# Windowed attention on one core: two slots for q and k, three for v and output, and a first q loaded as float32 by SyncE

## The chip, the core and the metric

The kernel runs on one core of a Trainium2 chip. The metric is the device time of one execution in microseconds (us). Executions of one kernel agree within about 0.3%; the change turns out to be of about that size, so the timed comparisons use interleaved rounds with a 95% interval. All timed runs quoted here are in the fast state (the record sets apart a slower state of the chip); the one run of a deliberately wrong kernel is a single one, of unknown state. "The span" is the length of the one execution that the profiler recorded. It is about 1.8 us shorter than the time of that execution (951.8 against 953.58 us for the kernel before).

## The reference, cut to what matters

```python
B, S, D = 4, 4096, 1536          # q, k, v: float32 [B, S, D]
W = 64                           # windows of 64 rows; a row attends to its own window only
logits = einsum('bnwd,bnud->bnwu', q_w, k_w) * D ** -0.5
attn = exp(logits - max); attn = attn / attn.sum(-1)
out = einsum('bnwu,bnud->bnwd', attn, v_w)      # float32 [B, S, D]
```

Three float32 inputs of 100.66 MB each are read once, one output of 100.66 MB is written once: 402.65 MB over HBM, whatever the kernel does.

## The kernel before

The 16384 rows are worked off in 32 units of 512 rows. A unit loads q, k and v (3.15 MB each in HBM) through the queue of POOL (GpSimd), which casts to float16 on the way. PE transposes q and k, multiplies them, ACT takes the exponential, PE multiplies with v, ACT and DVE scale the result into an output tile, and POOL stores that tile (3.15 MB). The last unit is cut into three parts (half, quarter, quarter) to shorten the end, and the three stores of its last part go through SP (SyncE).

```python
AHEAD = 2; SLOTS = 4
units = [Unit(i * UR, [(0, 4, 2)]) for i in range(N - 1)]
units.append(Unit((N - 1) * UR, [(0, 2, 2), (2, 3, 1), (3, 4, 1)]))
inp  = tc.tile_pool(name="inp",  bufs=AHEAD + 1)   # three slots each for q, k, v: 12 KB per partition a slot
outp = tc.tile_pool(name="outp", bufs=2)           # two output slots: 24 KB per partition each
...
load_all(units[0]); ...; load_all(units[1])        # q, k, v of a unit, all through POOL's queue
...
probe = consts.tile([16, 16, 192], FP32)           # 12 KB per partition
for ui, u in enumerate(units):
    if ui + AHEAD < N:
        load_all(units[ui + AHEAD])                # q, k, v of the unit two ahead
    n = ui - 12
    if 1 <= n <= 15 and n != 8:                    # 14 small loads, nothing reads them
        nc.gpsimd.dma_start(out=probe[:n, n, :w], in_=qf[0:n, :w])
    for i in range(len(u.parts)):
        for h, et in scores(u, i):                 # transposes, q k^T, exp
            values(u, i, h, et, last)              # et v, scaled into u.o; last part: stores by nc.sync
        if not last:
            store(u, i)                            # nc.gpsimd.dma_start(out <- u.o)
```

Two facts of the built program matter. POOL's instructions run in order, and the loads and stores on its queue share eight completion semaphores in turn, so the ninth transfer is issued only when the first has landed. And an output tile is written again only after its store has landed.

The softmax here doesn't subtract the row's maximum and nothing guards it: scores larger than these inputs give would overflow.

## Time and profile before

| | before |
|---|---|
| time, median of the first 3 runs | 954.06 us (953.35 to 955.11) |
| span of the profiled run | 951.8 us |
| DMA | 9 tenths or more in 39 of 40 slices |
| PE / DVE / ACT / POOL busy | 70% / 45% / 45% / 10% |
| one unit in the steady part | 29.17 us |

From the page of the kernel before: engine totals, the DMA row of the 40 slices (each digit is a tenth of busy share), two of the DMA queues (packets, MB, share of 16 engines), the HBM account, the shares of the chain of waits, and one line of the list of DMA issues (count, KB each, us to landing):

```profile
span 951.8 us, 12993 instructions
...
PE 668.1 (70%) x5624; PEld 439.5 (46%) x5624; DVE 424.8 (45%) x489; ACT 431.0 (45%) x610; POOL 91.6 (10%) x154
...
DMA  9999999999999999999999999999999999999996
...
q0 software_dynamic: 27824, 250.96, 100.6%
q8 instruction: 44, 0.72, 0.3%
...
HBM read 302.07 MB, written 100.66 MB: 423 GB/s over the span
...
DMA 63%; PE 13%; ACT 7%; another core or an unknown queue 7%; DVE 6%; issue 2%; POOL 1%; ACTq 0%; POOLq 0%; DVEq 0%
...
out_dram<-out_sb POOLq DMA_DIRECT2D x31, 3072.0 KB, 44.0
```

The DMA row says what bounds the kernel. The HBM line gives the work: 402.7 MB. The trace records 16 semaphore updates for each DMA. They are read here as one for each of the 16 DMA engines, as its share lands; the trace doesn't name the engine. The loads of v of units 11, 12 and 13 land at 337.25, 366.42 and 395.58 us, so a unit's 12.58 MB (9.44 read, 3.15 written) take 29.17 us, which is 431 GB/s. At that rate 402.7 MB take 934 us, so at most 18 us of the span are not plain transfer. Note the trap in the chain: 47% of it is waiting for output stores, because that is what the compute engines wait for; but as long as the DMA queue is never empty, such waits cost no time.

The same semaphore updates show a second thing. The 16 engines do not stay together: from the first engine's landing to the last engine's, the very first load takes 1.3 us and the store of unit 30 takes 8.0 us (931.00 to 938.99 us).

The end, from the timeline (start us, duration us, engine, line, operation, out<-in; in brackets the idle time before it and what ended it):

```profile
917.87 1.02 PE L199 MATMUL o<-v,et 128*128 128x512 f16 x4
...
931.79 0.69 ACT L205 ACTIVATE out_sb<-o,rs 128x512 f32<-128x512 f32 x1 [14.09 <-DMA out_dram<-out_sb]
931.81 0.75 DVE L207 TENSOR_SCALAR out_sb<-o,rs 128x512 f32<-128x512 f32 x1 [13.60 <-DMA out_dram<-out_sb]
932.53 3.72 PE L199 MATMUL o<-v,et 128*128 128x512 f16 x8 [13.64 <-ACT out_sb L205]
...
937.60 0.54 POOL L214 DMA_DIRECT2D out_dram<-out_sb  x1 [23.07 <-DVE xq L141]
...
943.17 0.54 POOL L214 DMA_DIRECT2D out_dram<-out_sb  x1 [5.03 <-ACT out_sb L205]
...
947.48 1.49 SPq L210 DMA_DIRECT2D out_dram<-out_sb  x3
...
947.92 0.69 ACT L205 ACTIVATE out_sb<-o,rs 128x512 f32<-128x512 f32 x1 [0.47 <-PE o L199]
```

Line 199 is et times v, lines 205 and 207 are the scaling into the output tile, line 214 is a store by POOL and line 210 the last stores by SP. The first values of the last unit are ready at 918.9 us, but ACT and DVE must wait 14 us for an output slot; it comes free when the store of unit 29 lands (931.68 us on the last engine). After that the last unit's stores come as compute delivers them (937.6, 943.2, 947.5 us), and in between the DMA engines have nothing left: the store issued at 937.60 lands on all 16 engines between 942.77 and 942.94 us.

The view of waits gives the total of such waits (us, times, longest):

```profile
DVE out_sb L207 <- DMA out_dram<-out_sb: 48.0, 19, 13.6
...
ACT out_sb L205 <- DMA out_dram<-out_sb: 30.0, 16, 14.1
```

The start, from the timeline:

```profile
1.25 0.68 POOL L79 DMA_DIRECT2D q<-in_q_dram  x1 [0.81 <-POOLq L245]
1.92 0.56 POOL L79 DMA_DIRECT2D k<-in_k_dram  x1
...
12.21 4.37 PE L135 MATMUL tp<-ident,q 128*128 128x128 f16 x40 [12.21 <-DMA q<-in_q_dram]
```

The q load is POOL's first issue; PE starts when q has landed, at 12.2 us; k lands at 19.4 us.

### The profile page before, as it was taken

Reading aid. Unit: us, or ns where it says so; the run is one execution under the profiler, and the core shown is the slowest. Engines: PE = TensorE matmul, PEld = TensorE weight load, DVE = VectorE, ACT = ScalarE, POOL = GpSimd, SP = SyncE. Lnnn points to the kernel's source line nnn. Section 1 sums busy time; section 2 is a strip of 40 time slices with the busy share of each in tenths; the row PEclk is TensorE's granted clock in tenths of the full one; section 3 lists DMA queues with packets and bytes.
Section 4 is the critical chain, followed back from the end, with each engine's and each line's share of the span. In section 5 each row is a group of like instructions: output and inputs, shape, how many; then the busy total and the mean of one; then the engine's idle time right before and its main releaser. Section 6 shows DMA issues by size and latency. Waiting matters only on the chain.

```text
span 951.8 us, 12993 instructions
## 1 busy us (share of the span) xinstructions
PE 668.1 (70%) x5624; PEld 439.5 (46%) x5624; DVE 424.8 (45%) x489; ACT 431.0 (45%) x610; POOL 91.6 (10%) x154
## 2 busy tenths in 40 slices
PE   3777777768677677776676767767768668677644
PEld 3454445435454354553354544445445445344522
DVE  2554544544345443455434554434454345443422
ACT  2555544354444444444544345544354443454423
POOL 2101001010011000100011001100010101010000
PEclk9999989888799798899988889989798998898987
DMA  9999999999999999999999999999999999999996
GB/s 185 218 223 268 283 280 281 241 254 284 282 281 258 241 280 283 282 270 237 269 283 282 278 243 256 282 282 282 255 250 275 282 281 263 249 268 282 280 284 255
DMA packets 28313, 252.57 MB, mean 265 GB/s; under 512 B 2545, under 2 KB 2656, under 8 KB 12256
## 3 DMA queue, kind: packets, MB, share of 16 engines
q0 software_dynamic: 27824, 250.96, 100.6%
q8 instruction: 44, 0.72, 0.3%
q1 hardware_dynamic: 432, 0.79, 0.2%
q14 instruction: 13, 0.11, 0.0%
HBM read 302.07 MB, written 100.66 MB: 423 GB/s over the span
## 4 chain that ended last, share of the span: by engine, by line
DMA 63%; PE 13%; ACT 7%; another core or an unknown queue 7%; DVE 6%; issue 2%; POOL 1%; ACTq 0%; POOLq 0%; DVEq 0%
DMA out_dram<-out_sb 47%; DMA q<-in_q_dram 9%; PE o L199 8%; DMA k<-in_k_dram 7%; PE lt L148 3%; ACT out_sb L205 3%; DVE out_sb L207 3%; PE tp L135 3%; ACT et L174 2%; ACT xk L141 2%; DVE xk L141 2%; DVE xq L141 1%; ACT xq L141 0%; POOL out_dram L214 0%
## 5 line engine op out<-in xcount | busy, mean ns | idle before, releaser
L199 PE MATMUL o<-v,et 128*128 128x512 f16 x762 | 237.6, 420 | 91.2 <-ACT out_sb L205 86.8
L148 PE MATMUL lt<-xq,xk 128*128 128x256 f16 (+1 forms) x1536 | 232.6, 302 | 43.2 <-DVE xk L141 27.9
L207 DVE TENSOR_SCALAR out_sb<-o,rs 128x512 f32<-128x512 f32 x191 | 143.4, 751 | 197.7 <-PE o L199 149.7
L141 ACT COPY xk<-tp 128x1024 f16<-128x1024 f16 (+1 forms) x96 | 123.5, 1287 | 233.8 <-PE tp L135 233.8
L205 ACT ACTIVATE out_sb<-o,rs 128x512 f32<-128x512 f32 x193 | 132.6, 687 | 158.7 <-PE o L199 118.0
L141 DVE COPY xk<-tp 128x1024 f16<-128x1024 f16 (+1 forms) x97 | 123.3, 1271 | 178.6 <-PE tp L135 178.6
L148 PEld LDWEIGHTS <-xk 128*128 128x128 f16 x1536 | 151.9, 108 | 92.3 <-DVE xk L141 41.7
L135 PE MATMUL tp<-ident,k 128*128 128x128 f16 x1536 | 130.8, 239 | 66.4 <-DMA k<-in_k_dram 60.1
L199 PEld LDWEIGHTS <-et 128*128 128x128 f16 x762 | 74.0, 101 | 220.3 <-issue 183.3
L141 DVE COPY xq<-tp 128x1024 f16<-128x1024 f16 (+1 forms) x129 | 152.2, 1255 | 12.6 <-PE tp L135 12.5
L135 PEld LDWEIGHTS <-k 128*128 128x128 f16 x1536 | 113.3, 109 | 78.4 <-DMA k<-in_k_dram 68.3
L135 PE MATMUL tp<-ident,q 128*128 128x128 f16 x1536 | 103.7, 221 | 37.9 <-DVE xq L141 21.8
L141 ACT COPY xq<-tp 128x1024 f16<-128x1024 f16 x64 | 82.1, 1283 | 91.4 <-PE tp L135 91.4
L135 PEld LDWEIGHTS <-q 128*128 128x128 f16 x1536 | 93.2, 99 | 54.4 <-issue 34.6
L174 ACT ACTIVATE et<-lt,zeros 32x128 f16<-32x128 f32 (+1 forms) x256 | 91.6, 358 | 33.0 <-PE lt L148 27.4
L192 DVE RECIPROCAL rs<-sp 128x2 f32<-128x2 f32 (+1 forms) x65 | 10.7, 165 | 133.1 <-PE sp L187 133.1
L214 POOL DMA_DIRECT2D out_dram<-out_sb x33 | 23.8, 720 | 391.2 <-DVE out_sb L207 269.9
L187 PE MATMUL sp<-ones,et 128*128 128x1 f16 x254 | 16.4, 167 | 41.1 <-ACT et L174 41.1
L187 PEld LDWEIGHTS <-et 128*128 128x128 f16 x254 | 14.3, 102 | 61.8 <-ACT et L174 50.3
L79 POOL DMA_DIRECT2D v<-in_v_dram x34 | 23.6, 694 | 180.8 <-DMA out_dram<-out_sb 51.1
L79 POOL DMA_DIRECT2D q<-in_q_dram x34 | 18.6, 546 | 114.1 <-DMA probe<-in_q_dram 53.1
L79 POOL DMA_DIRECT2D k<-in_k_dram x34 | 18.6, 547 | 78.2 <-DMA k<-in_k_dram 37.2
(11 smaller groups left out, 10.1 us busy)
## 6 DMA issues: line engine op xcount, KB each, us to landing
out_dram<-out_sb POOLq DMA_DIRECT2D x31, 3072.0 KB, 44.0
q<-in_q_dram POOLq DMA_DIRECT2D x31, 1536.0 KB, 47.7
k<-in_k_dram POOLq DMA_DIRECT2D x31, 1536.0 KB, 50.8
v<-in_v_dram POOLq DMA_DIRECT2D x31, 1536.0 KB, 51.3
out_dram<-out_sb POOLq DMA_DIRECT2D x1, 1536.0 KB, 5.3
q<-in_q_dram POOLq DMA_DIRECT2D x1, 768.0 KB, 46.9
k<-in_k_dram POOLq DMA_DIRECT2D x1, 768.0 KB, 43.2
v<-in_v_dram POOLq DMA_DIRECT2D x1, 768.0 KB, 46.4
```

What stands on the lines that cost most here:

```text
L79: nc.gpsimd.dma_start(out=dst, in_=rows(src, u.first[i], hi - lo, r))
L135: nc.tensor.transpose(tp[:, (c - c0) * R + r, j, :], src[:, lo + R * j + r, c * P : (c + 1) * P], ident,)
L141: copy(out=dst, in_=tp)
L148: nc.tensor.matmul(lts[h][:, r, :, :], lhsT=kc[:, r, h, :], rhs=qc[:, :, h, :], start=(c == 0 and r == 0), stop=(c == DC - 1), skip_group_ ...
L174: nc.scalar.activation(et[s, :, :, s], lts[h][s, :, :, s], EXP, bias=zeros[s], scale=scale)
L187: nc.tensor.matmul(sp[:, t, 0:1], lhsT=et[:, r, t, :], rhs=ones[:, 0:1], start=(r == 0), stop=(r == R - 1),)
L192: nc.vector.reciprocal(out=rs, in_=sp[:, :, 0])
L199: nc.tensor.matmul(o, lhsT=et[:, r, t, :], rhs=u.v[:, lo + R * h + r, sl], start=(r == 0), stop=(r == R - 1),)
L205: nc.scalar.activation(dst, o, COPY, bias=0.0, scale=rs[:, t : t + 1])
L207: nc.vector.tensor_scalar_mul(dst, o, scalar1=rs[:, t : t + 1])
L214: nc.gpsimd.dma_start(out=rows(of, u.first[i], hi - lo, R), in_=slots(u.o, lo, hi, R))
```

## The change

The intent: input and output slots are redistributed (q and k lose one slot each, output gains one), so that a store that has not landed stops nobody; k and q are reloaded as soon as a unit's scores are done; v is reloaded at the end of a unit for the third unit on, which is the same place in the program's order as before; and the very first load starts earlier, through SP, whose queue the profile lists as hardware_dynamic (POOL's is software_dynamic). This load is written without a cast, so q comes as float32 into an output slot that is still free, and DVE and ACT cast it. The probe loads go.

```diff
-    inp = ctx.enter_context(tc.tile_pool(name="inp", bufs=AHEAD + 1))
+    qkp = ctx.enter_context(tc.tile_pool(name="qkp", bufs=2))
+    vp = ctx.enter_context(tc.tile_pool(name="vp", bufs=3))
-    outp = ctx.enter_context(tc.tile_pool(name="outp", bufs=2))
+    outp = ctx.enter_context(tc.tile_pool(name="outp", bufs=3))
 ...
-    load_all(units[0])
+    raw = outp.tile([P, SLOTS, D], FP32, tag="out_sb", name="raw")
+    nc.sync.dma_start(out=slots(raw, 0, SLOTS, SLOTS), in_=rows(qf, 0, SLOTS, SLOTS))
+    load_all(0, "kv")
 ...
-    for u in units[1:AHEAD]:
-        load_all(u)
+    load_all(1, "qkv")
+    load_all(2, "v")
+    units[0].q = qkp.tile([P, SLOTS, D], FP16, tag="q16", name="q16")
+    for i in range(SLOTS):
+        copy = nc.scalar.copy if i % 2 else nc.vector.tensor_copy
+        copy(out=units[0].q[:, i, :], in_=raw[:, i, :])
 ...
-    probe = consts.tile([16, 16, 192], FP32, name="probe")
-
     for ui, u in enumerate(units):
-        if ui + AHEAD < N:
-            load_all(units[ui + AHEAD])
-        ... the 14 probe loads ...
         for i in range(len(u.parts)):
-            for h, et in scores(u, i):
+            blocks = scores(u, i)
+            if i == 0:
+                load_all(ui + 2, "qk")
+            for h, et in blocks:
                 values(u, i, h, et, last)
             if not last:
                 store(u, i)
+        load_all(ui + 3, "v")
```

More of the change, by code (lines that the diff above doesn't have):

```diff
@@ L26, in __init__ @@
         self.first = [row0 + P * lo for lo, hi, R in parts]
-AHEAD = 2
 SLOTS = 4
@@ L74, in load @@
         if not hasattr(u, name):
-            setattr(u, name, inp.tile([P, SLOTS, D], FP16, tag=name + "16", name=name + "16"))
+            pool = vp if name == "v" else qkp
+            setattr(u, name, pool.tile([P, SLOTS, D], FP16, tag=name + "16", name=name + "16"))
         src = {"q": qf, "k": kf, "v": vf}[name]
@@ L79, in load, with load_all @@
         nc.gpsimd.dma_start(out=dst, in_=rows(src, u.first[i], hi - lo, r))
-    def load_all(u):
-        for i in range(len(u.parts)):
-            for name in "qkv":
-                load(u, i, name)
-    load_all(units[0])
+    def load_all(ui, names):
+        if ui < N:
+            for i in range(len(units[ui].parts)):
+                for name in names:
+                    load(units[ui], i, name)
+    raw = outp.tile([P, SLOTS, D], FP32, tag="out_sb", name="raw")
+    nc.sync.dma_start(out=slots(raw, 0, SLOTS, SLOTS), in_=rows(qf, 0, SLOTS, SLOTS))
+    load_all(0, "kv")
     ident = consts.tile([P, P], FP16, name="ident")
@@ L214, in store @@
         nc.gpsimd.dma_start(out=rows(of, u.first[i], hi - lo, R), in_=slots(u.o, lo, hi, R))
-    probe = consts.tile([16, 16, 192], FP32, name="probe")
     for ui, u in enumerate(units):
-        if ui + AHEAD < N:
-            load_all(units[ui + AHEAD])
-        n = ui - 12
-        if 1 <= n <= 15 and n != 8:
-            w = 128 + 4 * n
-            nc.gpsimd.dma_start(out=probe[:n, n, :w], in_=qf[0:n, :w])
         for i in range(len(u.parts)):
             last = ui == N - 1 and i == len(u.parts) - 1
-            for h, et in scores(u, i):
+            blocks = scores(u, i)
+            if i == 0:
+                load_all(ui + 2, "qk")
+            for h, et in blocks:
                 values(u, i, h, et, last)
```

## The prediction

> **What bounds the kernel now.** The DMA engines. The page's slices show DMA at 9 tenths in 39 of 40 slices, against PE 70%, DVE and ACT 45% of the span. The page's HBM line gives 302.07 MB read plus 100.66 MB written. In the steady part one unit (9.4 MB read, 3.1 MB written) takes 29.17 us between landings, 431 GB/s (worked out from the trace's landing times). The Trainium skill ("DMA: Bandwidth & Descriptors", section "Where 436 GB/s comes from") puts the fabric ceiling at 435 GB/s; this trace agrees to 1%. 402.7 MB at 431 GB/s is 934 us, so at most 18 us of the 951.8 us span can be saved. They lie, by packets and landings: about 3.7 us at the start; the 16 engines drift apart (first to last landing of one DMA grows from 1.3 to 8.0 us), and the last engine decides; after 939 us the queue runs dry twice while the last unit is still being computed.
>
> **That tail is what the change can touch.** The timeline shows unit 31's first value matmuls done at 918.9 us; then ACT waits 14.1 us and DVE 13.6 us for the store of unit 29 to land (931.7 us), because there are only two output slots. PE stands still with them. Stores land 44 us after issue (list of DMA issues), so output slots stall the middle too (chain of waits: 47% on output stores), but there the DMA queue never empties, so that costs nothing.
>
> **What the change does.**
> - Three output slots: unit 31 writes into unit 28's slot, free around 900 us. The 13.6 us stall goes; compute ends about 940-943 us instead of 948.6 us.
> - Two q/k slots, q/k loads issued after a unit's scores: less look-ahead, but about four 3 MB transfers (7.3 us each) stay queued, as a unit computes in 25 us unstalled against 29.2 us of DMA. No steady starvation. The program's order shows that unit 2's q waits for unit 0's transposes only.
> - First q through SyncE as float32: the same 3.1 MB read. It shares the 16 engines with k (same page, "Issuing engines are not separate DMA queues"), so q and k land together at 17-18 us instead of 12.2 and 19.4; then casts of a few us. First transposes about 20-21 us instead of 12.2. Not critical: over 50 us of loads are queued. Data starts about 1 us earlier.
> - The small probe loads (14, under 80 KB) go: about 0.5 us in total.
>
> **Sum.** Slowest DMA engine: 939 us, minus 1 (start), minus 0.5 (probes), plus the last unit's 3.1 MB store 7.3 us, plus about 1 us end = 946 us. Compute: unit 30 ends about 916, the parts of unit 31 take 13, 6 and 6.5 us, last store 2.3 us: about 945. Both meet at a span near 946 us, time about 948 us: 0.6% faster. Range 945 to 951.5 us. Faster by over 2%: 0.02; within 2%: 0.96; slower by over 2%: 0.02.
>
> **What would show it.** Right: no wait of ACT/DVE for output stores near the end, DMA at full share until about 943 us, unit period still 29.2 us, first transposes near 20 us without a hole in the DMA share at 45-60 us.
>
> **What would make it wrong.** A DMA hole after the first loads if unit 0 starts much later; q/k slots released too late, so that PE waits for k and DMA idles; a lower PE clock in the tail; the engines' drift growing beyond 8 us.

## The result, and the profile after

The time is 949.83 us (median of 4 runs, 949.5 to 950.32) against 954.44 us (median of 4): ratio 0.9953, 95% interval 0.9936 to 0.997. Ratios are the mean time of one kernel's fast runs over that of the other's of the same rounds, so not quite the ratio of the medians. The change is 0.5% faster, and clear of noise.

The page after, the lines that answer to those above:

```profile
span 948.6 us, 12985 instructions
...
DMA  9999999999999999999999999999999999999997
...
q0 software_dynamic: 27232, 249.31, 100.2%
q1 hardware_dynamic: 576, 3.93, 1.1%
q8 instruction: 44, 0.72, 0.3%
...
HBM read 301.99 MB, written 100.66 MB: 424 GB/s over the span
...
out_dram<-out_sb POOLq DMA_DIRECT2D x31, 3072.0 KB, 41.9
```

The transfers are the same and the DMA row is as full. The small second queue (q1) now holds the first q (3.15 MB) beside the last stores.

The end of the changed kernel, from the timeline (lines 209, 215, 217 are the former 199, 205, 207; 224 and 220 are the stores):

```profile
927.10 1.02 PE L209 MATMUL o<-v,et 128*128 128x512 f16 x4
...
927.73 0.69 ACT L215 ACTIVATE out_sb<-o,rs 128x512 f32<-128x512 f32 x1 [0.80 <-PE o L209]
928.16 0.75 DVE L217 TENSOR_SCALAR out_sb<-o,rs 128x512 f32<-128x512 f32 x1 [0.72 <-PE o L209]
928.47 3.56 PE L209 MATMUL o<-v,et 128*128 128x512 f16 x8 [0.35 <-ACT out_sb L215]
...
933.39 0.55 POOL L224 DMA_DIRECT2D out_dram<-out_sb  x1 [12.19 <-DVE xq L151]
...
938.62 0.55 POOL L224 DMA_DIRECT2D out_dram<-out_sb  x1 [4.69 <-ACT out_sb L215]
...
942.93 1.49 SPq L220 DMA_DIRECT2D out_dram<-out_sb  x3
...
943.37 0.69 ACT L215 ACTIVATE out_sb<-o,rs 128x512 f32<-128x512 f32 x1 [0.47 <-PE o L209]
```

No wait of 14 us is left: the values of the last unit's first part are scaled as soon as PE delivers them, and the last part's scaling ends at 944.06 us instead of 948.61. The view of waits has one line that names an output store, and it is POOL waiting for one of its eight semaphores, not for a slot:

```profile
POOL q L80 <- DMA out_dram<-out_sb: 13.8, 2, 7.0
```

The start, from the timeline (line 91 is the first q by SP, line 114 the casts):

```profile
0.74 0.38 SPq L91 DMA_DIRECT2D raw<-in_q_dram  x1
...
1.26 0.67 POOL L80 DMA_DIRECT2D k<-in_k_dram  x1 [0.81 <-POOLq L251]
...
15.26 2.85 ACT L114 CAST q<-raw 128x1536 f16<-128x1536 f32 x2 [13.23 <-DMA raw<-in_q_dram]
15.26 1.83 DVE L114 CAST q<-raw 128x1536 f16<-128x1536 f32 x2 [14.30 <-DMA raw<-in_q_dram]
...
18.16 3.00 PE L145 MATMUL tp<-ident,q 128*128 128x128 f16 x29 [0.62 <-ACT q L114]
```

SP issues at 0.74 us; q lands at 15.24 us and k at 17.96 us instead of 12.16 and 19.44. Both together are there 1.5 us earlier, q alone 3 us later, which fits its sharing the engines with k (no run tests that by itself). PE's transposes run from 18.2 us on; nothing comes of that delay, since the DMA queue was filled far beyond.

The landings of the end, taken from the semaphore updates in the traces, all in us from the span's start. "Scaled" is the end of the last ACT instruction on the output tile:

| | before | after |
|---|---|---|
| store of unit 30: first engine / last engine | 931.00 / 938.99 | 930.57 / 939.70 |
| last output scaled | 948.61 | 944.06 |
| last store landed on all engines | 950.93 | 947.13 |
| end of the span | 951.8 | 948.6 |

So the changed kernel gains 4.6 us of compute at the end and 3.8 us at the last landing, while the slowest DMA engine is no earlier at all at the store of unit 30, in spite of the earlier start.

### The profile page after: what moved, and what is told of

It is laid out like the page before. It is cut to its first block, busy times and chain, and to the rows that moved or that the text cites. A ratio compares the mean times of both kernels' runs of the same rounds, so it can differ in the third digit from the quotient of the medians.

```text
span 948.6 us, 12985 instructions
## 1 busy us (share of the span) xinstructions
PE 666.8 (70%) x5624; PEld 443.1 (47%) x5624; DVE 426.9 (45%) x491; ACT 434.2 (46%) x612; POOL 83.7 (9%) x139
## 5 line engine op out<-in xcount | busy, mean ns | idle before, releaser
L209 PE MATMUL o<-v,et 128*128 128x512 f16 x762 | 226.8, 402 | 65.6 <-ACT out_sb L215 61.4
L158 PE MATMUL lt<-xq,xk 128*128 128x256 f16 (+1 forms) x1536 | 236.9, 306 | 41.4 <-DVE xk L151 25.9
L158 PEld LDWEIGHTS <-xk 128*128 128x128 f16 x1536 | 154.1, 110 | 92.3 <-DVE xk L151 39.0
L145 PE MATMUL tp<-ident,k 128*128 128x128 f16 x1536 | 136.4, 245 | 81.7 <-DMA k<-in_k_dram 78.4
L145 PEld LDWEIGHTS <-k 128*128 128x128 f16 x1536 | 118.1, 112 | 94.1 <-DMA k<-in_k_dram 83.2
L209 PEld LDWEIGHTS <-et 128*128 128x128 f16 x762 | 72.7, 99 | 188.1 <-issue 147.5
L197 PEld LDWEIGHTS <-et 128*128 128x128 f16 x254 | 13.6, 98 | 60.0 <-ACT et L184 50.4
```

What stands on the lines that cost most here:

```text
L145: nc.tensor.transpose(tp[:, (c - c0) * R + r, j, :], src[:, lo + R * j + r, c * P : (c + 1) * P], ident,)
L158: nc.tensor.matmul(lts[h][:, r, :, :], lhsT=kc[:, r, h, :], rhs=qc[:, :, h, :], start=(c == 0 and r == 0), stop=(c == DC - 1), skip_group_ ...
L197: nc.tensor.matmul(sp[:, t, 0:1], lhsT=et[:, r, t, :], rhs=ones[:, 0:1], start=(r == 0), stop=(r == R - 1),)
L209: nc.tensor.matmul(o, lhsT=et[:, r, t, :], rhs=u.v[:, lo + R * h + r, sl], start=(r == 0), stop=(r == R - 1),)
```

## The experiments

The theory was: the third output slot is what the change gains, by taking the wait for the store of unit 29 away; then the slowest DMA engine sets the end. Rivals: the early first q, the new order and slots of the loads, or the removal of the probe loads. All but experiment 5 were timed in five rounds against the kernel before, experiments 1 to 4 together on one chip, then 6 to 8 (with 5), then 9 to 11; "ratio" is always to the kernel before.

### 1. Third output slot alone, with the old loads

A third output slot fits beside nine input slots only if the 12 KB of the probe tile go (before that it didn't build, for want of 11 KB per partition). So this is the kernel before with a third output slot, minus the probes:

```diff
-    outp = ctx.enter_context(tc.tile_pool(name="outp", bufs=2))
+    outp = ctx.enter_context(tc.tile_pool(name="outp", bufs=3))
-    (probe tile and probe loads)
```

> The kernel before with a third output slot and without the probe loads (the probe tile's 12 KB per partition are what the third slot needs); three q/k/v slots, order of loads and first q through POOL as before. Theory (the third output slot is the gain): the 13.6 us wait for the store of unit 29 is gone, compute ends near 939-941 us, the slowest DMA engine then ends the kernel: about 938.5 + 7.3 + 1 = 947 us span, time about 948.7 us, ratio to before 0.994. Rival (early first q and look-ahead of q/k/v are the gain): only the probes' 0.5 us, time about 953.5 us, ratio 0.999.

Measured: 951.64 us, ratio 0.9972 (0.996 to 0.9985). That is between theory and rival: faster than before and clear of noise, but it missed my number by 3 us. The end of this run, from the timeline:

```profile
930.02 0.54 POOL L214 DMA_DIRECT2D out_dram<-out_sb  x1 [4.69 <-ACT out_sb L205]
...
934.33 1.61 SPq L210 DMA_DIRECT2D out_dram<-out_sb  x3
...
934.77 0.69 ACT L205 ACTIVATE out_sb<-o,rs 128x512 f32<-128x512 f32 x1 [0.46 <-PE o L199]
```

The wait is gone, as expected, but the sizes were off: the last output is scaled at 935.46 us, 13 us earlier than before and 3.5 us or more earlier than expected, which was of no use. The store of unit 30 lands 1.2 us later than the 938.5 us of the expectation, and the last store lands at 946.88 us, 7.2 us after it (939.68 us on the last engine). But the span ends at 949.9 us, 3.0 us after that landing, where the kernel before needed 0.9 us. In the sequencer's records POOL's closing drain, an instruction at the end of its program, runs from 930.00 to 949.11 us, and only then the closing barrier goes on. The last transfer of POOL's own queue, the store of the second part, had landed at 946.49 us. So the drain ended 2.6 us after POOL's last DMA. In the kernel before the two last events were further apart, POOL's last landing at 946.97 and SP's last at 950.93 us, and the drain was hidden.

### 2. The changed kernel with two output slots

```diff
-    outp = ctx.enter_context(tc.tile_pool(name="outp", bufs=3))
+    outp = ctx.enter_context(tc.tile_pool(name="outp", bufs=2))
```

> The changed kernel with two output slots again, all else kept. Theory: ACT and DVE wait again some 12 us or more for the store of unit 29 (lands near 932 us on the slowest engine), unit 31 ends some 19 us later, span 951-953 us, time 953-955 us, ratio to before 0.999-1.001. Rival: the gain stays, time about 950 us, ratio 0.995.

Measured: 954.07 us, ratio 0.9998 (0.9984 to 1.0012). The whole gain is gone with the slot. From the view of waits (the profile is of the fastest of the five runs, 952.63 us):

```profile
ACT out_sb L215 <- DMA out_dram<-out_sb: 7.7, 1, 7.7
DVE out_sb L217 <- DMA out_dram<-out_sb: 7.2, 1, 7.2
```

The wait is back, only shorter than expected (7 to 8 us, not 12), and ends at 931.2 us when the store of unit 29 lands (931.13 us on the last engine). The last output is scaled at 947.7 us, the last store lands at 949.98 us. The view has no other wait of ACT or DVE for an output store: the 19 and 16 such waits of the kernel before have shrunk to this one at the end, and yet the time is that of the kernel before. This settles the first part of the theory: the other parts of the change, without the third slot, are worth nothing that five rounds can see.

### 3. The changed kernel with the first q through POOL

```diff
-    raw = outp.tile(...); nc.sync.dma_start(out=raw, in_=q rows)
-    load_all(0, "kv")
+    load_all(0, "qkv")
-    (the four casts)
```

> The changed kernel with the very first q loaded by POOL with the cast in the DMA, as before. Theory: start is 0.7 to 1.5 us later, everything behind it shifts by that: time 950.5 to 951.3 us, ratio to before 0.996-0.997. Rival (the early float32 q is the gain): time about 954 us, ratio 1.000.

Measured: 951.29 us, ratio 0.9969 (0.9956 to 0.9981). k of unit 0 lands at 19.31 us instead of 17.96. The theory's upper end holds and the rival's 954 us does not; by the medians the early q is worth 1.5 us, or 0.9 us against the repeat in experiment 10. Taken by itself this is not clear of noise: the intervals of this run and of the changed kernel overlap. This kernel also differs from that of experiment 1 by the new order and slots of the loads alone, and in the same rounds it is 0.35 us faster by the medians (ratios 0.9969 and 0.9972): nothing that can be told from noise.

### 4. The kernel before without the probe loads

```diff
-    probe = consts.tile([16, 16, 192], FP32, name="probe")
-        if 1 <= n <= 15 and n != 8:
-            nc.gpsimd.dma_start(out=probe[:n, n, :w], in_=qf[0:n, :w])
```

> The kernel before without the probe loads, nothing else. Theory: 14 transfers of 0.05 to 0.2 us go: -0 to -1 us, time 953.4 to 954.4 us, ratio 0.999 to 1.000. Rival (a probe takes one of the eight semaphores of the queue, so without them the queue is deeper by one large transfer and everything gains): -2 us or more, ratio 0.998 or less.

Measured: 953.79 us, ratio 0.9996 (0.9983 to 1.0008). No effect that can be seen; the rival is out. The probes' only importance is the 12 KB that they occupy.

### 5. What drives the DMA engines apart: a short PE program

The slowest engine's lag of 8 to 10 us decides the end, so it deserved a test. The page lists a queue of kind "instruction" (q8) with 44 packets, 0.72 MB, 16 KB each. The program of PE has 11256 instructions. The Trainium skill ("Runtime: NRT & Kernel Launch", section "Instruction fetch mechanics") says that an engine's instruction memory is refilled in blocks of 16 KiB, 256 instructions, through a DMA queue: 11256 / 256 is 44, so these packets would be PE's program. In the trace of the changed kernel one such packet takes 0.88 to 0.98 us, and the spread between first and last engine grows in steps. Four of these steps:

| packet of q8, number and start | spread just before | spread just after |
|---|---|---|
| 17th, 364.1 us | 5.21 us | 6.33 us |
| 25th, 535.7 us | 5.86 us | 6.97 us |
| 33rd, 701.7 us | 6.96 us | 8.11 us |
| 41st, 875.5 us | 8.03 us | 9.19 us |

From the 17th on, every eighth packet sets the slowest engine back by 1.1 us. With the steps at the 1st and 9th packet these come to about 6.6 of the 8.5 us by which the spread grows (0.65 to 9.13 us); the rest, such as 1.0 us near the 13th packet, falls elsewhere. The kernel before is less regular: it steps by 0.8 to 1.3 us at its 9th, 17th, 25th and 33rd packets, not at its 41st, and by less at others. The experiment cuts PE's program and leaves every data transfer: only two of twelve column chunks are transposed and multiplied, so the result is wrong.

```diff
-        starts = list(range(0, DC, CG))
+        starts = [0]
-                        stop=(c == DC - 1),
+                        stop=(c == CG - 1),
```

> Wrong result on purpose: the changed kernel with only the first two of twelve column chunks transposed and multiplied, so PE's program is 3648 instructions instead of 11256 while every DMA stays. Theory (the drift of the DMA engines comes from fetches of PE's program, 44 packets of 16 KB that take 0.9 us each on a few of the 16 engines): about 14 such packets, the spread from first to last landing of the store of unit 30 falls from 9.1 us to 2 to 5 us, its last landing comes 4 to 7 us earlier (933 to 936 us) while the first landing stays at 930.6 us within 1 us. Rival (some engines are simply slower at their own transfers, or fall behind by the semaphore traffic): the spread stays at 8 to 9 us.

From the page of this run:

```profile
span 943.4 us, 4981 instructions
...
PE 413.1 (44%) x1820; PEld 177.1 (19%) x1820; DVE 224.3 (24%) x322; ACT 242.0 (26%) x463; POOL 83.7 (9%) x139
...
DMA  9999999999999999999999999999999999999997
...
q0 software_dynamic: 27232, 249.31, 100.5%
...
q8 instruction: 14, 0.23, 0.1%
...
HBM read 301.99 MB, written 100.66 MB: 427 GB/s over the span
```

Measured, in one look: 945.46 us. 14 fetch packets instead of 44; the store of unit 30 lands between 929.87 and 933.69 us, a spread of 3.8 us instead of 9.1. The slowest engine is 6.0 us earlier, the fastest 0.7 us. The theory holds and the rival does not. One reservation: PE, ACT and DVE do less as well (PE 44% busy instead of 70%, at a mean granted clock of 0.65 instead of 0.90), so the run alone doesn't exclude that quieter memories help. The steps in the table do not depend on that run, and it has one of its own: 2.8 to 3.9 us at its 9th packet (583.8 us), while its 5th to 8th leave the spread at 2.7 to 2.9 us.

### 6. Experiment 1 with the last unit's stores through SP

```diff
-        nc.gpsimd.dma_start(out=rows(...), in_=slots(u.o, lo, hi, R))
+        queue = nc.sync if u is units[-1] else nc.gpsimd
+        queue.dma_start(out=rows(...), in_=slots(u.o, lo, hi, R))
```

> The first experiment (before without probes, three output slots) with all stores of the last unit issued by SP instead of POOL. Theory (POOL's closing drain lasts until 2.6 us after the last transfer of its own queue, which ended that kernel): the drain then follows the store of unit 30 and is over near 942.5 us; last landing stays near 946.9 us, span 947.8 us, time 949.5 us, 2 us under the first experiment, ratio to before 0.9953. Rival (the drain is long for another reason, or the HW queue is slower): 951 us or more.

Measured: 950.46 us, ratio 0.9968 (0.9954 to 0.9981): half of the expected 2 us by the medians, and nothing by the ratio to before. The step that failed: POOL's last transfer, the store of unit 30, did not land at 939.7 us but at 945.26 us, because the stores on SP's queue took turns with it on the same engines. The Trainium skill ("DMA: Bandwidth & Descriptors", section "Queues, rings and completion order") says that each engine goes round its queues packet by packet, and this run agrees: the store of the second part, issued 15 us later, landed before it, at 941.46 us. POOL's drain then ended at 947.80 us, again 2.5 us after POOL's last landing, and the span at 948.6 us.

### 7. The changed kernel with the last unit's stores through SP

The same edit in the changed kernel.

> The changed kernel with all stores of the last unit issued by SP. Theory: only the 0.6 us go by which POOL's drain outlasted the last landing; compute still ends at 944 us: time 949.2 us, ratio 0.9947. Rival (the last stores on POOL's queue hold the tail up by more): 948 us or less.

Measured: 949.47 us, ratio 0.9952 (0.994 to 0.9965), last landing 946.81, span 947.7 us. The size is as the theory said, and too small to tell from the changed kernel; its step "compute still ends at 944 us" was not met, since the last output was scaled at 941.3 us, without the last landing following it.

### 8. Old slots and order, third output slot, early q, last stores through SP

```diff
+    raw = outp.tile(...); nc.sync.dma_start(out=raw, in_=q rows)     # as in the change
-    (probe tile and probe loads)
     inp bufs=3, outp bufs=3, order of loads as before; last unit's stores by nc.sync
```

> Before without probes, with three output slots, the first q through SP as float32 and the last unit's stores through SP; three q/k/v slots and the order of the loads as before. Theory: the early start is worth 0.7 to 1.5 us on top of the run with the last stores on SP: time 948.0 to 948.9 us, ratio 0.994 to 0.9947. Rival (two q/k slots and the new order of loads are worth something by themselves): not below the changed kernel's 949.8 us.

Measured: 949.90 us, ratio 0.9959 (0.9947 to 0.9972). It missed the expected range by 1 us and lies on the changed kernel's time. The last output is scaled at 935.7 us, 8 us earlier than in the changed kernel, and yet the last store lands at 946.01 us and POOL's drain ends at 947.1 us. So the theory's number failed and the rival's was met, but the rival is hardly shown by that. The fair comparison is experiment 7, which has the new order and slots and the same stores on SP, in the same rounds: 949.47 against 949.90 us, ratios 0.9952 and 0.9959 with intervals that overlap. So the new order shows 0.4 us, not clear of noise.

### 9. The store of unit 30 through SP too

On top of experiment 8:

```diff
-        queue = nc.sync if u is units[-1] else nc.gpsimd
+        queue = nc.sync if u in units[-2:] else nc.gpsimd
```

> The run with all three parts together, and the store of unit 30 through SP as well, so that POOL's queue ends with the last load (near 924-928 us) and its drain is over by 932 us. Theory (POOL's drain is what ended that kernel 1.1 us after its last landing): last landing stays near 946.0 us on the slowest DMA engine, which has the same bytes to move, span near 947.0 us, time 948.5 to 949.2 us, ratio 0.9945 to 0.995. Rival (the round-robin of the two queues puts the last loads off so far that compute ends the kernel): compute ends after 940 us and the time is not below 949.9 us.

Measured: 949.66 us, ratio 0.9953 (0.9941 to 0.9966). Here I had overlooked that the store of unit 29 stands behind the last loads in POOL's order: it landed at 944.79 us, so the drain was again the last, at 947.25 us. The last loads were put off as the rival said (v of the last part landed at 937.33 us, the last output was scaled at 941.5 us). Neither theory's reason is what was seen; the time is the same again.

### 10. The changed kernel once more

No edit; it ran beside experiments 9 and 11.

> The changed kernel itself, unchanged, on the same chip and in the same rounds: 949.8 us within 0.5 us, ratio 0.9953 within 0.0007.

Measured: 950.35 us, ratio 0.996 (0.9946 to 0.9974). The ratio fits; the median is 0.05 us outside. In this profile the last output was scaled at 940.88 us, 3.2 us earlier than in the first profile of the same kernel, and still the span was 949.6 us: the store of unit 30 landed at 940.02 us on the last engine, the last store at 947.46 us, POOL's last store at 946.25 us with its drain over at 948.83 us. Compute did not set this end.

### 11. The stores of units 29, 30 and 31 through SP

On top of experiment 8:

```diff
-        queue = nc.sync if u is units[-1] else nc.gpsimd
+        queue = nc.sync if u in units[-3:] else nc.gpsimd
```

> As the run before it, with the store of unit 29 through SP too. Both theories: that store overtakes some 45 us of queued loads, k of unit 30 lands 4 to 7 us later and compute ends 4 to 7 us later; if that stays under 943 us the time is the same as with two units, otherwise 1 to 3 us longer.

Measured: 952.32 us, ratio 0.9984 (0.9971 to 0.9996). The store of unit 29 overtakes the queued loads, the last load lands at 944.36 us and the last output is scaled at 947.4 us. Compute ends the kernel again and costs over 2 us, as expected of that case.

No version beat the changed kernel by more than the noise. By the medians experiments 7 and 9 lie 0.4 and 0.2 us below its first measurement and 0.9 and 0.7 us below the repeat in experiment 10; their ratios are inside its interval.

## Why the prediction was right, point by point

- **What bounds the kernel.** Right. The DMA row is full before and after, and a unit still takes 29.2 us after (the stores of units 12 and 13 land at 433.06 and 462.22 us). The comparison with 435 GB/s counts bytes in HBM; see the last list.
- **The tail stall is what can be gained; the third slot removes it.** Right, and shown by experiment 2: with two slots the stall and the whole 0.5% come back. The waits for output stores in the middle, 47% of the chain, were worth nothing, as predicted: the changed kernel has none of them, and its unit takes as long.
- **No starvation from fewer q and k slots, no hole after the first loads.** Right. The DMA share has no hole in any slice; q alone came earlier (15.2 us) than predicted (17 to 18 us), with no effect.
- **Probes 0.5 us.** Nothing could be seen (ratio 0.9996), which agrees.
- **The early start, 1 us.** By the landing of k of unit 0 the start was 0.8 us earlier on the first engine (17.31 us instead of 18.10) and 1.5 us on the last; the last engine is the poorer measure, since experiments 1 and 4, with the old start, have it at 18.87 and 18.96 us. Taking the early q away costs 0.9 to 1.5 us by the medians of experiments 3, 10 and the result, at the size of the noise.
- **The size.** Predicted 948 us, a gain of 0.6%; measured 949.8 us, 0.5%. The mechanism was right. The terms that were mis-sized are the first and the last of the sum for the slowest DMA engine: "939 us, minus 1 (start), minus 0.5 (probes)" and "plus about 1 us end". The first sum gives 937.5 us for the store of unit 30; it landed at 939.70 us on the last engine, 2.2 us later. Half of that is that the fastest engine was only 0.44 us earlier than before and not 1.5 us; the other half is the spread, 9.1 us and not the 8.0 I carried over. The prediction had named a drift beyond 8 us among what would make it wrong; it came, and took 1.1 us. In the correct runs whose store of unit 30 shared the engines with nothing on SP's queue, the spread was 8.0 to 10.0 us, so a value from one trace has an error of about 1 us. The second was 1.4 us (947.13 to 948.55), as POOL's drain ended 0.7 us after the last landing. The middle term held everywhere: in four correct runs whose compute was early enough, the last landing comes 7.2 to 7.4 us after the last engine's landing of the store of unit 30 (939.70 and 947.13 in the changed kernel; 939.68 and 946.88; 940.98 and 948.42; 940.02 and 947.46 in experiments 1, 3 and 10), which is the last unit's 3.15 MB at full rate, 7.3 us.

How the 0.5% is made up, by the ratios: the third slot with the old order 0.28%, and the early start and the new order the rest, which is at the size of the noise. Without the third slot the rest showed nothing (experiment 2), so the parts do not simply add. What stays open: which engines take the instruction fetches, why the steps come at every eighth one, and whether the new order of the loads is worth anything at all (0.35 and 0.4 us in two pairs of runs, not clear of noise). Once the stall is gone, every arrangement but that of experiment 11 ended at the same wall, the slowest DMA engine at 946.0 to 948.4 us plus the end of the program (POOL's drain and the barrier), and the experiments cannot rank them.

## What to carry to other kernels

When the DMA engines are always busy, ask only what happens before the first and after the last full slice: a wait that fills half of the chain in the middle was worth nothing, and one of 14 us at the end was the whole gain. Take the end from the landing on the slowest DMA engine, not from the average rate, and add what that engine still has to move. Before moving the last stores to another queue, write down which transfer then is last on each queue, because they share the engines and the closing drain follows the last one of POOL's.

## What the Trainium skill lacked or had wrong

- "Runtime: NRT & Kernel Launch", section "Instruction fetch mechanics", calls the cost of crossing a 16 KiB block mostly hidden. For PE it may be; in a kernel bound by DMA it is not: each block took 0.88 to 0.98 us of a DMA engine, the slowest engine fell back by 1.1 us at every eighth one from the 17th on, and with 14 blocks instead of 44 the slowest engine was 6.0 us earlier (experiment 5, which also did less compute).
- "DMA: Bandwidth & Descriptors", section "Latency and other measured facts", says that engines 7 and 15 are usually slower and guesses at the descriptor rings. No run here shows which engines were slow, but most of the spread of 8 to 10 us grew at instruction fetches, in steps, which points to another cause here.
- No page says that POOL's closing drain lasts until after POOL's own transfers: in twelve of the thirteen profiles it ended 2.4 to 2.6 us after the last landing on POOL's own queue (four of them: 946.49 to 949.11, 945.26 to 947.80, 944.55 to 947.06, 946.25 to 948.83 us), in the kernel before 3.0 us after it (946.97 to 950.00 us), and up to 2.2 us of that were added to the span where no store of SP was later.
- "DMA: Bandwidth & Descriptors", section "Where 436 GB/s comes from", states a ceiling of 435 GB/s, and 431 GB/s were measured, but the two do not count the same bytes. The section puts the ceiling at the ports of SBUF, and there the loads arrive cast to half their size: the page of the kernel before counts 250.96 MB on POOL's queue against 402.7 MB in HBM. The section also says that for transfers between HBM and SBUF the HBM side, about 358 GB/s, binds; this one core moved 431 GB/s of HBM traffic. Which limit the kernel meets is not shown.
